# Weaving the last head's recurrence with the key and value expansion, in an order pinned on TensorE

## The chip, the cores and the metric

One NeuronCore of a Trainium2 chip runs the whole kernel. The metric is the device time of one execution in microseconds (us). Three runs of the kernel before took 884.52, 885.75 and 885.99, a median of 885.75.

## What is computed

One layer of a diffusion backbone over 640 tokens: 512 latent ones and 128 of context, five blocks of 128. One input projection feeds two groups of heads side by side. The part that matters here, shortened:

```python
hm, C_new, n_new, m_new = _mlstm_bidir(mq, mk, mv, gates_i, gates_f, ctx_C, ctx_n, ctx_m)   # 4 heads x 128
hm = _rmsnorm(hm, mlstm_norm_g) * sigmoid(mo)
ckv = _rmsnorm(kv_lat, kv_lora_g)                              # 256 wide
q = _mla_queries(q_lat, q_lora_g, w_q_up, q_head_g, rope)      # 384 wide -> 8 heads x 96
kv = (ckv @ w_kv_up).reshape(B, T, 8, 64 + 64)                 # the key and value expansion
k, v = rmsnorm(concat(kv[..., :64], k_rope)), kv[..., 64:]     # also for 128 cached context tokens
ha = _block_attention(q, k, v)
x = x + g1 * (concat(hm, ha) @ w_out)                          # then the feed-forward layer
```

The recurrence of a head is computed chunkwise: scores s of a block's keys with all queries, times decay weights W, give p; numerators are sums of p times v over blocks, forward and backward, and end in a normalised quotient hm. It does not depend on the expansion, nor the expansion on it.

## The kernel before

Weights and activations are split into a high and a low half, and three matmuls (high-high, high-low, low-high) make one product (`mm3`, L485-488). `split` (L108-110) makes the halves: a cast on ScalarE (L109) and a subtraction on VectorE (L110).

PSUM has two pools: psD, two buffers of two banks each (1024 columns), and psS, four buffers of one bank. A tile is written by TensorE and read by ScalarE and VectorE, and its buffer is then used again.

A framework orders the instructions: each engine has one queue, filled at build time by a list scheduler that takes whichever instruction is ready by its model, with the program's order as the priority. On the chip each engine takes its own queue strictly in order and waits at semaphores.

The stage around the change, in the program's order:

- `mlstm(h)` (L683-747): for j = 4 (context), 0, 1, 2, 3 the scores s (psS, three matmuls), for j < 4 the product c with the initial state (L716 scales it into the numerators num on ScalarE), the weights W (GpSimd adds the mask, L729; ScalarE takes exponentials, L730 and L732), p on VectorE (L739), and the forward numerator n (L698-706: matmuls L702, VectorE adds to num, L704, or ScalarE copies, L706). After the loop come the backward numerators.
- `context` (L749-764): a transpose pk, weighted keys kw on ScalarE (L757), the state pc (L760), its copy co and two output DMAs.
- `mlstm_end(h)` (L766-790): VectorE makes den (L770-772), hm in five blocks of 128 columns (L779, L780); ScalarE squares each with its sum (L781, into dg); VectorE scales the sums ssh (L782), GpSimd takes the root (rsh, L361), VectorE multiplies (L787), TensorE transposes (ht, hc, L788), VectorE multiplies by the output gate (L789, L790). It runs as a hook in `mlstm(h + 1)` after j = 0.
- After all four heads and `mlstm_end(3)`: the transposes ckt of the compressed latent and its halves kth and ktl (L806-815), then the expansion (L834-863): two halves hf of six tiles kvu of 128 tokens by 512 columns, six matmuls each, each tile in a psD buffer of its own. ScalarE copies the keys kn (L848), casts v (L109) or copies the context's v (L852), squares the keys (L854); VectorE makes the low half of v (L110) and sums the squares (L855). At the end of a half comes a reciprocal root on VectorE by iteration (L367-372).
- The query transposes qlt (L870), their split into qth and qtl, and the query product qu (L486-488). Strips of the modulation matrix w_ada (L389) fill TensorE from here on; their loads go through SyncE's queue in an order fixed at build time.

Of the kernel before, what the change touches and what calls it, by code (L numbers as in the profile page):

```python
# [19 lines left out]
P = 128  # L20
# [34 lines left out]
def hybrid_layer(ctx: ExitStack, tc: tile.TileContext, d, o):  # L55
# [429 lines left out]
    def mm3(out, lh, ll, rh, rl, start, stop):  # L485
        PE.matmul(out, lhsT=lh, rhs=rh, start=start, stop=False)  # L486
        PE.matmul(out, lhsT=lh, rhs=rl, start=False, stop=False)
        PE.matmul(out, lhsT=ll, rhs=rh, start=False, stop=stop)
# [194 lines left out]
    def mlstm(h, hook=None):  # L683
# [7 lines left out]
        def blk(dr, j, i):  # L691
            if i == 4:
                return pc_[:, dr, :]
            s0 = off[dr][j] + (i - j if dr == 0 else i) * P
            return pu[:, dr, s0:s0 + P]


        def numer(dr, i):  # L698
            js = [4] if i == 4 else (list(range(i + 1)) if dr == 0 else list(range(i, 4)))
            ps = psS(f"n{h}{i}{dr}")[:, 0:VC]  # L700
            for j in js:
                PE.matmul(ps, lhsT=blk(dr, j, i), rhs=mv32[:, j, h, :], start=j == js[0], stop=j == js[-1])  # L702
            if i < 4:
                V.tensor_tensor(out=num[dr][:, i, :], in0=ps, in1=num[dr][:, i, :], op=ALU.add)  # L704
            else:
                S.copy(num[dr][:, i, :], ps)  # L706

        wc = sm("wc", [P, 2], bufs=2)
        for j in (4, 0, 1, 2, 3):
            s_ps = psS(f"s{h}{j}")  # L710
            if j < 4:
                mm3(s_ps, kh[:, j * P:(j + 1) * P], kl_[:, j * P:(j + 1) * P], qh[:, 0:TL], ql_[:, 0:TL], True, True)
                pc = psS(f"c{h}{j}")[:, 0:260]
                mm3(pc, qh[:, j * P:(j + 1) * P], ql_[:, j * P:(j + 1) * P], ch, cl, True, True)
                for dr in range(2):
                    S.activation(out=num[dr][:, j, :], in_=pc[:, dr * 130:dr * 130 + VC], func=AF.Copy, scale=w_col[:, j, dr, h:h + 1])  # L716
            else:
                mm3(s_ps[:, 0:P], kh[:, TL:T], kl_[:, TL:T], qh[:, TL:T], ql_[:, TL:T], True, True)
# [21 lines left out]
            numer(0, j)  # L740
            if j == 4:
                numer(1, 4)
                context(h, kc, wc)
            if j == 0 and hook:
                hook()
        if h + 1 < MH:
            mlstm_loads(h + 1)
        for i in (3, 2, 1, 0):
            numer(1, i)  # L749
        fin[h] = (num, sg)  # L750

    def context(h, kc, wc):
        pk = psS(f"pk{h}")[:, 0:P]
        PE.transpose(out=pk, in_=kc, identity=ident)
# [4 lines left out]
        for dr in range(2):  # L759
            PE.matmul(pc[:, dr * 130:dr * 130 + VC], lhsT=kw[:, dr, :], rhs=mv32[:, 4, h, :], start=True, stop=True)  # L760
# [73 lines left out]
    for hf in range(2):  # L834
        ku = U(f"kn{hf}")
        kn = view(ku, 0, 6, 4, QK)
        vu = U(f"v{hf}", F32R)
        vv = view(vu, 0, 5, 4, P)
        hi, lo = wget(("kup", hf))
        ssk = sm("ssk", [P, 6, 4], bufs=1)  # L840
        rsk = sm("rsk", [P, 6, 4], bufs=1)
        for i in range(6):
            ps = psD(f"kvu{hf}{i}")[:, 0:512]
            for k in range(2):
                c = slice(k * 512, (k + 1) * 512)
                mm3(ps, kth[:, k, i * P:(i + 1) * P], ktl[:, k, i * P:(i + 1) * P], hi[:, c], lo[:, c], k == 0, k == 1)
            p4 = ps.rearrange("p (h c) -> p h c", h=4)
            S.copy(kn[:, i, :, 0:NOPE], p4[:, :, 0:NOPE])  # L848
            if i < 5:
                split(vv[:, i, :, 0:VD], vv[:, i, :, VD:P], p4[:, :, NOPE:P])  # L850
            else:
                S.copy(vctx[:, hf], p4[:, :, NOPE:P])  # L852
            sq = view(Pp(f"sqk{hf}{i}"), 0, 4, NOPE)
            S.activation(out=sq, in_=kn[:, i, :, 0:NOPE], func=AF.Square)  # L854
            V.tensor_reduce(out=ssk[:, i, :], in_=sq, axis=AX.X, op=ALU.add)  # L855
        V.tensor_tensor(out=ssk, in0=ssk, in1=ssr.unsqueeze(2).broadcast_to([P, 6, 4]), op=ALU.add)
        V.tensor_scalar(out=ssk, in0=ssk, scalar1=1.0 / QK, scalar2=EPS, op0=ALU.mult, op1=ALU.add)
        rsqrt_v(rsk.rearrange("p a b -> p (a b)"), ssk.rearrange("p a b -> p (a b)"))
        for k in range(4):
            G.tensor_tensor(out=kn[:, :, k, 0:NOPE], in0=kn[:, :, k, 0:NOPE], in1=rsk[:, :, k:k + 1].broadcast_to([P, 6, NOPE]), op=ALU.mult)  # L860
            G.tensor_tensor(out=kn[:, :, k, NOPE:QK], in0=krr, in1=rsk[:, :, k:k + 1].broadcast_to([P, 6, ROPE]), op=ALU.mult)
        kn_u.append(kn)
        v_u.append(vv)
# [551 lines left out]
```

## Time and profile before

| | us |
|---|---|
| median of 3 runs | 885.75 |
| profiled execution | 885.93 |
| its span | 883.8 |
| its time outside the span | 2.13 |

The first part of the page gives the busy time of each engine and its share of the span. A row of the windows has the stretch, its length, busy time and count of TensorE (PE), its weight loads (PEld), VectorE (DVE), ScalarE (ACT) and GpSimd (POOL), then the granted TensorE clock, where 1.00 is full, the DMA engines' busy share and GB/s. A row of the waits names the engine and line that waited, for whom, the total in us, how often, and the longest. A row of a timeline has its start from the span's beginning, its duration, engine, line, operation, output and inputs, shapes and how many alike stand in it (x5); in brackets stands the idle time of the engine before it and what ended it. TensorE overlaps its matmuls, so that they start closer together than one lasts.

### The profile page before, as it was taken

To read this page: it belongs to the slowest core of one execution; us is meant where nothing else is said; L and a number is where in the kernel's file an instruction comes from. 1 tells how busy PE (TensorE), PEld (TensorE's weight loads), DVE (VectorE), ACT (ScalarE), POOL (GpSimd) and SP (SyncE) were. 2 spreads that over 40 slices of the span, in tenths; PEclk is the share of its full clock that TensorE was granted. 3 is DMA by queue.
4 is the path that set the end of the run, shared out by engine and by line. 5 is a ranking of instruction groups with operands and counts; after the bars stand their busy time and mean duration, and the time that the engine had idled before them with its cause. 6 is when DMAs were issued, how large, how long until landed. Compare 5 with 4: busy or idle time off the path is not lost.

```text
span 883.8 us, 15202 instructions
## 1 busy us (share of the span) xinstructions
PE 856.6 (97%) x5805; PEld 801.8 (91%) x5805; DVE 615.9 (70%) x1226; ACT 436.6 (49%) x959; POOL 297.2 (34%) x301
## 2 busy tenths in 40 slices
PE   6999999999889999999989999999999999999998
PEld 5689889999778677889989999999999999999998
DVE  2654733646787889977898587595876949678663
ACT  3424425545864688955557253361544517254540
POOL 3100113322333576743753152241514215152300
PEclk9999999999999999999999999999999999999999
DMA  9742853231316200322141312122122221412132
GB/s 358 307 145 61 281 185 89 63 102 48 99 57 239 96 1 1 120 72 72 49 144 45 99 49 96 49 96 96 49 96 88 80 73 57 134 50 73 48 102 90
DMA packets 22328, 89.63 MB, mean 101 GB/s; under 512 B 3144, under 2 KB 3944, under 8 KB 18928
## 3 DMA queue, kind: packets, MB, share of 16 engines
q1 hardware_dynamic: 19440, 81.95, 26.8%
q0 software_dynamic: 1664, 4.26, 1.7%
q10 hardware_dynamic: 1152, 2.46, 0.7%
q8 instruction: 46, 0.75, 0.4%
q14 instruction: 26, 0.21, 0.1%
HBM read 85.33 MB, written 3.32 MB: 100 GB/s over the span
## 4 chain that ended last, share of the span: by engine, by line
PE 84%; DVE 8%; DMA 3%; ACT 3%; issue 1%; POOL 0%; SPq 0%; DVEq 0%; ACTq 0%; POOLq 0%
PE dn L637 25%; PE qk L637 6%; PE wo L637 5%; PE mo L637 3%; PE ada L389 2%; PE pv L1013 2%; DMA st<-in_w_ada 2%; PE n L702 2%; PE up8M L1235 1%; PE up12M L1235 1%; PE up13M L1235 1%; PE up15M L1235 1%; PE up14M L1235 1%; PE up11M L1235 1%; PE up9M L1235 1%; PE up7M L1235 1%
## 5 line engine op out<-in xcount | busy, mean ns | idle before, releaser
L109 ACT CAST wh<-st 128x1024 fp32r<-128x1024 f32 (+4 forms) x69 | 69.3, 1007 | 101.1 <-PE dn L637 32.9
L1118 DVE SCALAR_TENSOR_TENSOR xr<-dn,modT,xr 128x320 f32<-128x320 f32 x64 | 35.3, 551 | 107.3 <-PE dn L637 107.3
L637 PE MATMUL dn<-fh,wh 128*128 128x320 f32 x448 | 102.7, 310 | 0.2 <-ACT fh L1278 0.2
L110 DVE TENSOR_TENSOR wl<-st,wh 128x1024 fp32r<-128x1024 f32 (+4 forms) x67 | 83.3, 1246 | 27.8 <-ACT wh L109 26.8
L637 PE MATMUL dn<-fh,wl 128*128 128x320 f32 x448 | 102.0, 309 | 0.0
L637 PE MATMUL dn<-fl,wh 128*128 128x320 f32 x448 | 98.7, 309 | 0.0
L109 ACT CAST wu<-S 128x512 fp32r<-128x512 f32 x64 | 38.1, 616 | 98.5 <-issue 92.3
L637 PEld LDWEIGHTS dn<-fh,wh 128*128 128x128 f32 x448 | 74.8, 188 | 2.1 <-PE dn L637 1.6
L637 PEld LDWEIGHTS dn<-fh,wl 128*128 128x128 f32 x448 | 75.0, 188 | 0.0
L637 PEld LDWEIGHTS dn<-fl,wh 128*128 128x128 f32 x448 | 74.1, 188 | 0.0
L1273 POOL TENSOR_TENSOR r<-r,rbs 128x320 f32<-128x320 f32 x32 | 37.4, 1180 | 106.9 <-DVE r L1251 106.9
L110 DVE TENSOR_TENSOR wu<-S,wu 128x512 fp32r<-128x512 f32 x64 | 57.4, 906 | 1.1 <-ACT wu L109 0.9
L1277 ACT ACTIVATE r<-r 128x192 f32<-128x192 f32 (+2 forms) x96 | 40.8, 465 | 26.0 <-DVE r L1251 17.1
L729 POOL TENSOR_TENSOR W<-ngb,mask 128x128 f32<-128x128 f32 x40 | 19.5, 501 | 66.5 <-DVE p L739 33.2
L1280 DVE TENSOR_TENSOR fl<-r,fh 128x320 fp32r<-128x320 f32 x56 | 38.1, 699 | 3.0 <-ACT r L1279 3.0
L1004 POOL TENSOR_TENSOR tot<-tot,p 128x512 f32<-128x512 f32 x24 | 37.2, 1550 | 5.9 <-ACT p L986 3.9
L109 ACT CAST wu<-pair 128x512 fp32r<-128x512 f32 x24 | 14.1, 615 | 43.8 <-PE dn L637 41.6
L110 DVE TENSOR_TENSOR pu<-p,pu 128x512 fp32r<-128x512 f32 x32 | 33.0, 1046 | 2.5 <-ACT pu L109 2.5
L219 POOL TENSOR_TENSOR S<-st,st 128x512 f32<-128x512 f32 x8 | 13.0, 1627 | 60.1 <-DVE wu L110 60.1
L1013 PE MATMUL pv<-pu,v 128*128 128x512 f32 x80 | 29.1, 427 | 2.1 <-DVE pu L110 2.0
L637 PE MATMUL wo<-mh,wh 128*128 128x320 f32 x128 | 29.6, 311 | 0.7 <-DVE xr L1120 0.7
L637 PE MATMUL qk<-hh,wl 128*128 128x320 f32 x128 | 29.9, 312 | 0.0
(487 smaller groups left out, 2437.6 us busy)
## 6 DMA issues: line engine op xcount, KB each, us to landing
st<-in_w_ada SPq DMA_DIRECT2D x16, 1024.0 KB, 5.4
st<-in_w_down SPq DMA_DIRECT2D x32, 512.0 KB, 3.4
ad<-in_w_ada SPq DMA_DIRECT2D x8, 1024.0 KB, 17.2
st<-in_w_up SPq DMA_DIRECT2D x16, 512.0 KB, 3.7
pair<-in_w_up SPq DMA_DIRECT2D x16, 512.0 KB, 4.9
st<-in_w_qko SPq DMA_DIRECT2D x12, 512.0 KB, 3.6
st<-in_w_out SPq DMA_DIRECT2D x8, 512.0 KB, 3.5
x<-in_x SPq DMA_DIRECT2D x4, 640.0 KB, 6.8
```

Of the source, the lines that this page charges most:

```text
L109: S.copy(hi, src)
L110: return eng.tensor_tensor(out=lo, in0=src, in1=f(hi), op=ALU.subtract)
L389: PE.matmul(ps[32 * j:32 * j + 32, 0:n], lhsT=sz[:, 2 * q + k, :], rhs=w[:, k, c], start=q == 0, stop=q == 3, tile_position=(0, 32 * j))
L637: PE.matmul(out[:, hf * 512:hf * 512 + HT], lhsT=wt[:, c], rhs=xt[k][:, hf * HT:(hf + 1) * HT], start=k0 == 0 and n == 0, stop=k1 == nk an ...
L729: G.tensor_tensor(out=W[:, dg:dg + P], in0=nb_[dr][:, j * P:(j + 1) * P], in1=mask[:, dr, :], op=ALU.add)
L1004: G.tensor_tensor(out=tot[h], in0=first, in1=pj, op=ALU.add)
L1013: PE.matmul(pacc[h], lhsT=v_u[hf][:, j, hh_, :], rhs=w, start=j == 0 and k == 0, stop=j == 4 and k == 1)
L1118: V.scalar_tensor_tensor(out=xr[m][:, 0:HT], in0=ps[:, 0:HT], scalar=modT[:, gi_ + m, 0:1], in1=xr[m][:, 0:HT], op0=ALU.mult, op1=ALU.add)
L1235: PE.matmul(ps, lhsT=w[:, c], rhs=b[k], start=k == 0 and w is hi and b is bh, stop=k == 3 and w is lo)
L1273: E.tensor_tensor(out=t, in0=t, in1=rbs[:, c], op=ALU.mult)
L1277: S.activation(out=t[:, c0:c1], in_=t[:, c0:c1], func=AF.Relu, bias=r[n][:, w:w + 1])
L1280: V.tensor_tensor(out=FL[n][:, c], in0=t, in1=f(FH[n][:, c]), op=ALU.subtract)
```

## The change

The expansion becomes a generator, `expand()`, which stops after each tile. `mlstm` of the last head gets it as `fill` and takes one tile after each of its steps j = 4, 0, 1, 2, 3, and one in the backward numerators after i = 2. With `fill`, the forward numerator of a step is computed one step later (`due`); `context` is cut into `context` and `context_out`, and the second is another step later. `queued()` puts each of these matmul groups behind the one before it on TensorE (`issue_after`), so that the scheduler can't take them in another order; `line.clear()` ends that, and the remaining tiles follow without it. Two tiles share a double bank of psD, one in each half. ckt, krr and what belongs to them move ahead of the last head's recurrence in the program, `mlstm_end(3)` behind it.

```diff
-    def mlstm(h, hook=None):
+    line = {}
+
+    def queued():
+
+        return tc.issue_after(line["pe"].ins) if line else nullcontext()
+
+    def mlstm(h, hook=None, fill=None):
...
             ps = psS(f"n{h}{i}{dr}")[:, 0:VC]
-            for j in js:
-                PE.matmul(ps, lhsT=blk(dr, j, i), rhs=mv32[:, j, h, :], start=j == js[0], stop=j == js[-1])
+            with queued():
+                for j in js:
+                    last = PE.matmul(ps, lhsT=blk(dr, j, i), rhs=mv32[:, j, h, :], start=j == js[0], stop=j == js[-1])
+            if fill:
+                line["pe"] = last
...
         wc = sm("wc", [P, 2], bufs=2)
+        due = None
         for j in (4, 0, 1, 2, 3):
...
+            if due is not None:
+                numer(0, due)
+                if due == 4:
+                    numer(1, 4)
+                    kw = context(h, kc, wc)
+                elif due == 0:
+                    context_out(h, kw)
...
-            numer(0, j)
-            if j == 4:
-                numer(1, 4)
-                context(h, kc, wc)
+            if fill:
+
+                due = j
+                fill()
+            else:
+                numer(0, j)
+                if j == 4:
+                    numer(1, 4)
+                    context_out(h, context(h, kc, wc))
             if j == 0 and hook:
                 hook()
         if h + 1 < MH:
             mlstm_loads(h + 1)
+        if fill:
+            numer(0, due)
         for i in (3, 2, 1, 0):
             numer(1, i)
+            if fill and i == 2:
+                fill()
         fin[h] = (num, sg)
...
+        return kw
+
+    def context_out(h, kw):
         pc = psS(f"pc{h}")
...
-    for h in range(MH):
+    for h in range(MH - 1):
         mlstm(h, (lambda: mlstm_end(h - 1)) if h else None)
-        if h + 1 < MH:
-            head_in(h + 1)
-    mlstm_end(MH - 1)
+        head_in(h + 1)
...
-    for hf in range(2):
...
-        for i in range(6):
-            ps = psD(f"kvu{hf}{i}")[:, 0:512]
...
+    def expand():
+
+        for hf in range(2):
...
+            for i in range(6):
+                if i % 2 == 0:
+                    pair = psD(f"kvu{hf}{i}")
+                ps = pair[:, i % 2 * 512:i % 2 * 512 + 512]
+                with queued():
+                    for k in range(2):
+                        c = slice(k * 512, (k + 1) * 512)
+                        last = mm3(ps, kth[:, k, i * P:(i + 1) * P], ktl[:, k, i * P:(i + 1) * P], hi[:, c], lo[:, c], k == 0, k == 1)
+                if line:
+                    line["pe"] = last
...
+                if i < 5:
+                    yield
...
+    tiles = expand()
+    mlstm(MH - 1, lambda: mlstm_end(MH - 2), lambda: next(tiles))
+    line.clear()
+    mlstm_end(MH - 1)
+    for _ in tiles:
+        pass
```

What it does to the queues shows at three places. The names are the tiles of above with the head and step appended (s31 is the score of head 3, j = 1; ht2 and hc2 are the transposes of head 2's hm), wh and wl the halves of weights.

TensorE before, around the last transposes of head 2. Ahead of this piece stand seven tiles of the expansion (kvu00 to kvu05 and kvu10), head 3's s30, c30, context and first numerators, and the first three transposes, which come between kvu10 and kvu11.

```order
L486 MATMUL kvu11_2747<-wh32_2280,kth_2567 128x512
L487 MATMUL kvu11_2747<-wl32_2281,kth_2567 128x512
L488 MATMUL kvu11_2747<-wh32_2280,ktl_2568 128x512
L788 MATMUL ht2_2421<-ident_94,hm2_2400 128x128
L788 MATMUL hc2_2422<-ident_94,hm2_2400 128x128
L486 MATMUL s31_2435<-mqk3_2160 128x512
L487 MATMUL s31_2435<-mqk3_2160 128x512
L488 MATMUL s31_2435<-mqk3_2160 128x512
L486 MATMUL c31_2439<-chl3_2139,mqk3_2160 128x260
```

TensorE after, the same transposes. Ahead of this piece stand s34, the first tile, s30, c30, the numerators n340 and n341, and pk3; the second tile bears its pair's name, kvu00.

```order
L486 MATMUL kvu00_2413<-wh31_2221,kth_2336 128x512
L487 MATMUL kvu00_2413<-wl31_2222,kth_2336 128x512
L488 MATMUL kvu00_2413<-wh31_2221,ktl_2337 128x512
L828 MATMUL ht2_2494<-ident_94,hm2_2473 128x128 x4
L828 MATMUL hc2_2495<-ident_94,hm2_2473 128x128
L486 MATMUL s31_2508<-mqk3_2160 128x512
L487 MATMUL s31_2508<-mqk3_2160 128x512
L488 MATMUL s31_2508<-mqk3_2160 128x512
```

The transposes moved from around the eighth tile to behind the second, and the third to twelfth tile and all of the recurrence's steps from s31 on now stand behind them.

ScalarE before, from the first square (dg) of head 2 to the fourth of its five.

```order
L781 ACTIVATE dg_2403,ssh_2401<-hm2_2400 128x128
L716 ACTIVATE num30_2338<-c30_2377,cols_1009 128x129
L716 ACTIVATE num31_2339<-c30_2377,cols_1009 128x129
L781 ACTIVATE dg_2403,ssh_2401<-hm2_2400 128x128 x2
L848 COPY kn0_2615<-kvu02_2651 128x4x64
L109 CAST v0_2616<-kvu02_2651 128x4x64
L732 ACTIVATE W310_2445<-ngb0_2131,cols_1009 128x256
L762 COPY co_2369<-pc3_2366 128x2x129
L781 ACTIVATE dg_2403,ssh_2401<-hm2_2400 128x128
L732 ACTIVATE W311_2450<-ngb1_2133,cols_1009 128x128
L732 ACTIVATE W320_2469<-ngb0_2131,cols_1009 128x128
```

ScalarE after, from the copy of the second tile to the fifth square.

```order
L893 COPY kn0_2403<-kvu00_2413 128x4x64
L109 CAST v0_2404<-kvu00_2413 128x4x64
L821 ACTIVATE dg_2476,ssh_2474<-hm2_2473 128x128
L899 ACTIVATE sqk01_2465<-kn0_2403 128x256
L821 ACTIVATE dg_2476,ssh_2474<-hm2_2473 128x128 x2
L754 ACTIVATE W310_2528<-ngb0_2131,cols_1009 128x256
L754 ACTIVATE W311_2533<-ngb1_2133,cols_1009 128x128
L821 ACTIVATE dg_2476,ssh_2474<-hm2_2473 128x128
L752 ACTIVATE W310_2528<-W310_2528,cols_1009 128x128
L752 ACTIVATE W311_2533<-W311_2533,cols_1009 128x128
L821 ACTIVATE dg_2476,ssh_2474<-hm2_2473 128x128
```

The squares now stand closer together; the exponentials L754 and L752 of W310 and W311 (L732 and L730 before) stand between the third, the fourth and the fifth.

TensorE before, behind the last tile of the expansion: the query transposes qlt0 to qlt2, and ht3 and hc3, the transposes of head 3's hm.

```order
L870 MATMUL qlt0_2835<-ident_94,ql_u_1038 128x128 x5
L788 MATMUL ht3_2553<-ident_94,hm3_2532 128x128 x2
L870 MATMUL qlt1_2845<-ident_94,ql_u_1038 128x128 x5
L788 MATMUL ht3_2553<-ident_94,hm3_2532 128x128 x2
L788 MATMUL hc3_2554<-ident_94,hm3_2532 128x128
L870 MATMUL qlt2_2855<-ident_94,ql_u_1038 128x128 x5
```

TensorE after, the same piece; kvu14 is the pair of the last two tiles, and its second half stands here.

```order
L926 MATMUL qlt0_2829<-ident_94,ql_u_1038 128x128 x5
L828 MATMUL ht3_2707<-ident_94,hm3_2686 128x128 x4
L828 MATMUL hc3_2708<-ident_94,hm3_2686 128x128
L486 MATMUL kvu14_2781<-wh32_2280,kth_2336 128x512
L487 MATMUL kvu14_2781<-wl32_2281,kth_2336 128x512
L488 MATMUL kvu14_2781<-wh32_2280,ktl_2337 128x512
```

The last tile and the last two query transposes moved behind all of head 3's transposes.

## Rows read from the trace of the kernel before

**Rows 1.** The page: span, and busy time by engine.

```profile
span 883.8 us, 15202 instructions
PE 856.6 (97%) x5805; PEld 801.8 (91%) x5805; DVE 615.9 (70%) x1226; ACT 436.6 (49%) x959; POOL 297.2 (34%) x301
```

**Rows 2.** Windows: the stretch of the recurrence's first steps.

```profile
229.00:246.50 17.50, 14.84 (x76) 11.93 (x75) 14.08 (x51) 13.81 (x52) 5.41 (x9) 1.00 0.24 79
```

**Rows 3.** Waits of TensorE, 226 to 300 us.

```profile
PE kvu L486 <- DVE v L110: 2.8, 3, 1.3
PE pc L760 <- ACT kw L757: 1.4, 1, 1.4
...
PE qlt L870 <- ACT qlt L872: 0.6, 1, 0.6
PE ada L389 <- DMA st<-in_w_ada: 0.6, 2, 0.5
...
PE n L702 <- DVE p L739: 0.2, 1, 0.2
```

**Rows 4.** Timeline of TensorE, 229 to 267 us.

```profile
229.41 0.45 PE L486 MATMUL kvu<-wh,kth 128*128 128x512 f32 x1
...
232.68 0.27 PE L754 MATMUL pk<-ident,kc 128*128 128x128 f32 x1
...
234.60 0.48 PE L486 MATMUL s<-mqk 128*128 128x512 f32 x1
...
235.74 0.40 PE L486 MATMUL kvu<-wh,kth 128*128 128x512 f32 x1
...
244.67 0.49 PE L788 MATMUL ht<-ident,hm 128*128 128x128 f32 x3
...
265.55 0.44 PE L486 MATMUL qu<-wh,qth 128*128 128x384 f32 x1
```

**Rows 5.** Timeline of VectorE, 229.5 to 246 us.

```profile
233.26 1.06 DVE L779 TENSOR_SCALAR hm<-ck_u,den 128x128 f32<-128x128 f32 x5
234.24 0.42 DVE L110 TENSOR_TENSOR v<-kvu,v 128x256 fp32r<-128x256 f32 x1
...
236.02 0.60 DVE L780 SCALAR_TENSOR_TENSOR hm<-ck_u,den,hm 128x128 f32<-128x128 f32 x2
...
236.87 0.88 DVE L739 SCALAR_TENSOR_TENSOR p<-s,W 128x512 f32<-128x512 f32 x2
...
241.65 0.16 DVE L782 TENSOR_SCALAR ssh<-ssh 128x5 f32<-128x5 f32 x1
...
243.14 1.06 DVE L787 TENSOR_SCALAR hm<-hm,rsh 128x128 f32<-128x128 f32 x5
```

**Rows 6.** Timeline of ScalarE, 229.5 to 246 us.

```profile
232.21 0.37 ACT L848 COPY kn<-kvu 128x256 f32<-128x256 f32 x1 [2.06 <-PE kvu L488]
...
235.80 0.35 ACT L781 ACTIVATE dg<-hm 128x128 f32<-128x128 f32 x1
...
239.77 0.69 ACT L730 ACTIVATE W<-W,cols 128x128 f32<-128x128 f32 x2
```

**Rows 7.** Timeline of GpSimd, 229.5 to 246 us.

```profile
237.63 1.29 POOL L729 TENSOR_TENSOR W<-ngb,mask 128x128 f32<-128x128 f32 x3 [5.49 <-DVE p L739]
...
241.90 1.20 POOL L361 TENSOR_TENSOR rsh<-ssh,mhalf 128x5 f32<-128x5 f32 x1 [1.46 <-DVE ssh L782]
```

**Rows 8.** Windows: the end of the program.

```profile
880.00:882.50 2.50, 0.00 (x0) 0.00 (x0) 0.99 (x3) 0.00 (x0) 0.00 (x0) 1.00 0.37 131
882.50:883.80 1.30, 0.00 (x0) 0.00 (x0) 0.00 (x0) 0.00 (x0) 0.00 (x0) 0.53 0.00 0
```

**Rows 9.** Timeline of TensorE: strips at the start, and the last matmul.

```profile
16.44 3.64 PE L389 MATMUL ada<-ad,sz 128*32 128x256 f32 x32
...
22.79 1.93 PE L389 MATMUL ada<-ad,sz 128*32 128x256 f32 x32
...
879.51 0.31 PE L637 MATMUL dn<-f,wl 128*128 128x320 f32 x1
```

More of the change, by code (lines that the diff above doesn't have):

```diff
@@ L1 @@
-from contextlib import ExitStack
+from contextlib import ExitStack, nullcontext
 import numpy as np
@@ L487, in mm3 @@
         PE.matmul(out, lhsT=lh, rhs=rl, start=False, stop=False)
-        PE.matmul(out, lhsT=ll, rhs=rh, start=False, stop=stop)
+        return PE.matmul(out, lhsT=ll, rhs=rh, start=False, stop=stop)
     def group_n(keys, kts, ncol, name, nada=0):
@@ L711, in mlstm @@
             if j < 4:
-                mm3(s_ps, kh[:, j * P:(j + 1) * P], kl_[:, j * P:(j + 1) * P], qh[:, 0:TL], ql_[:, 0:TL], True, True)
-                pc = psS(f"c{h}{j}")[:, 0:260]
-                mm3(pc, qh[:, j * P:(j + 1) * P], ql_[:, j * P:(j + 1) * P], ch, cl, True, True)
+                with queued():
+                    mm3(s_ps, kh[:, j * P:(j + 1) * P], kl_[:, j * P:(j + 1) * P], qh[:, 0:TL], ql_[:, 0:TL], True, True)
+                    pc = psS(f"c{h}{j}")[:, 0:260]
+                    last = mm3(pc, qh[:, j * P:(j + 1) * P], ql_[:, j * P:(j + 1) * P], ch, cl, True, True)
+                if fill:
+                    line["pe"] = last
                 for dr in range(2):
@@ L717, in mlstm @@
             else:
-                mm3(s_ps[:, 0:P], kh[:, TL:T], kl_[:, TL:T], qh[:, TL:T], ql_[:, TL:T], True, True)
+                last = mm3(s_ps[:, 0:P], kh[:, TL:T], kl_[:, TL:T], qh[:, TL:T], ql_[:, TL:T], True, True)
+                if fill:
+                    line["pe"] = last
+            if due is not None:
[5 more added lines that the diff above has]
+                    context_out(h, kw)
             for dr in range(2):
@@ L753, in context @@
         pk = psS(f"pk{h}")[:, 0:P]
-        PE.transpose(out=pk, in_=kc, identity=ident)
+        with queued():
+            last = PE.transpose(out=pk, in_=kc, identity=ident)
+        if line:
+            line["pe"] = last
         kw = view(wwp.tile([P, 512], F32, tag="W", name=f"kw{h}"), 0, 2, P)
@@ L757, in context @@
             S.activation(out=kw[:, dr, :], in_=pk, func=AF.Copy, scale=wc[:, dr:dr + 1])
+        return kw
+    def context_out(h, kw):
         pc = psS(f"pc{h}")
-        for dr in range(2):
-            PE.matmul(pc[:, dr * 130:dr * 130 + VC], lhsT=kw[:, dr, :], rhs=mv32[:, 4, h, :], start=True, stop=True)
+        with queued():
+            for dr in range(2):
+                last = PE.matmul(pc[:, dr * 130:dr * 130 + VC], lhsT=kw[:, dr, :], rhs=mv32[:, 4, h, :], start=True, stop=True)
+        if line:
+            line["pe"] = last
         co = view(sm("co", [P, 260], bufs=1), 0, 2, 130)
@@ L832, in hybrid_layer @@
     V.tensor_copy(out=identr, in_=ident)
-    for hf in range(2):
[L835 to L841, printed above, removed]
-        for i in range(6):
-            ps = psD(f"kvu{hf}{i}")[:, 0:512]
[L844 to L863, printed above, removed]
```

30 lines of the change are left out of this document (added).

## The prediction

> **What bounds the kernel now.** The page's first part comes first: TensorE is busy 97% of the span [rows 1], so a change saves only where TensorE stands still, and costs wherever it newly does. The windows come next: of the 17.5 us from 229.0 TensorE works 14.84 [rows 2], so 2.66 us are idle at full clock. The waits of TensorE from 226 to 300 say for whom: the kv tiles for VectorE's low half of v, 2.8 us in three waits, pc for ScalarE's kw 1.4, the query transposes 0.6, a numerator 0.2, together 5.0, and weight strips for their DMA 0.6 [rows 3]. The timelines then give the dates. All this is what the change can win: 5.6 us of 885.93.
>
> **What moves.** TensorE takes its instructions in order, and that order is the one shown above: nothing later passes a waiting transpose. It differs from 229.4, the first kv tile, to about 296, and is the same behind. No matmul is added or removed: 72 matmuls of the twelve kv tiles, head 3's scores and numerators and the transposes only change places. So the sum is over waits.
>
> **A. The transposes of head 2, +6.2.** Before, eight kv tiles stand ahead of the last of these transposes, and they begin at 244.67 without a wait [rows 4]. Now two tiles stand there. When does TensorE arrive? Before, two tiles and the two context numerators take it from 229.41 to pk at 232.68, 3.27 us; s30 and c30 take from 234.60 to 235.74, 1.14 us [rows 4]. Now the same pieces and pk (0.3) lead up to ht2: 229.41 + 3.27 + 1.14 + 0.3 = 234.1, with 0.4 of small waits (under C) 234.5.
>
> When are its inputs there? VectorE began the five scalings hm at 233.26; now the v low half of the first tile, 0.42, stands ahead: 233.7, done by 234.7 (1.06 less the overlap); five accumulations at 0.26 (two took 0.60 with 0.08 of overlap) end at 236.0 [rows 5]. Then ScalarE squares the five blocks. In its new order two exponentials of W310 and W311 stand between the fourth square and the fifth, and they need GpSimd's masked sums. GpSimd started these 0.76 after VectorE's p had started (236.87 to 237.63) and took 1.29 for three [rows 5, 7]; p now starts at 236.0, since no tile's work stands between the accumulations, so the sums run from 236.8 to 238.0, the two exponentials after the second of them take 0.69 [rows 6] and end at 238.3, the last square, 0.35, and the read-out of its sum (0.2, an estimate) bring 238.9. From there the trace has the whole tail: ssh at 241.65, rsh at 241.90 for 1.20, hm times rsh at 243.14 [rows 5, 7], which is 1.49 from ssh to the scalings, and 0.3 until the first block is written (a fifth of their 1.06, and a signal). 238.9 + 1.49 + 0.3 = 240.7: TensorE stands from 234.5 to 240.7, **6.2 us**. If ScalarE took every square at once, the last would be done at 236.5, ht2 would start at 238.3, and the wait is 3.8: that is the low end. No reason leads below it, as the accumulations themselves end at 236.0. The high end is 7.0: ScalarE also casts, copies and squares the second tile in this stretch. I take 6.2. Behind ht2 stand s31, c31 and all the rest; nobody else fills the time, since tiles three to eight are queued behind it.
>
> **B. The waits of before, -5.0.** All of rows 3 but the DMA's go: the instructions that waited now stand elsewhere, with other suppliers.
>
> **C. New waits behind, +4.3.** The pairing looks like four buffers, but a tile is released as a whole: the second half of each double bank waits until VectorE has read the first. Ahead of ht2: pk 0.35 (ScalarE's copies of the numerators now come behind the first tile's kn, v and square) and the second tile 0.1. After ht2 the recurrence fills in well: only the fourth tile waits, 0.2. When the recurrence is out of steps, kvu13 waits for the v low half of kvu12, which stands on VectorE behind parts of two long chains, the root of the key norms and head 3's denominators: 0.9, the size that the same wait has (the kv row's 2.8 in three, the longest 1.3, mean 0.93). Head 3's transposes now stand ahead of kvu15 and wait 0.8 for the same kind of chain as head 2's; kvu15 0.2. qlt1 wants the double bank that kvu15 has just filled, so two ScalarE copies of 0.37 [rows 6] and their signals stand between: 0.9. The third query transpose and the first query tile wait for ScalarE's copies and casts: 0.9 together, where 0.6 was before. Sum 0.35 + 0.1 + 0.2 + 0.9 + 0.8 + 0.2 + 0.9 + 0.9 = 4.35, say 4.3. The low end is what the old order's tail had, one mean kv wait for each half and the query's: 0.93 + 0.93 + 0.6 = 2.4; the high end 5.5, if each of the last five is 0.25 longer. So the query product starts 6.2 - 5.0 + 4.3 = 5.5 after its 265.55 [rows 4], near 271.0.
>
> **D. Weight strips, -0.6.** The w_ada loads keep their time, since on SyncE's queue the next one even moves ahead of the load of w_q_up, while TensorE comes 5 us later: the two DMA waits, 0.6 [rows 3], are then over. From 0 to -0.6; I take -0.6.
>
> **E. TensorE's clock, +1.5.** [...]
>
> [...]
>
> **The sum.** 6.2 - 5.0 + 4.3 - 0.6 + 1.5 = 6.4 on the profiled execution's 885.93 (span 883.8 and 2.13 around it): 892.3. That execution is 0.18 above the median of 885.75, so I say **892.1**.
>
> **The rivals.**
> First, the clock stays up: all but E holds, 885.75 + 4.9 = **890.7**. For it: no dip between two matmuls in this trace. Against: a fall 2.7 us after the last one.
> [...]
> Third, ScalarE reaches the squares as they come: A is 3.8 and C 2.4: 3.8 - 5.0 + 2.4 - 0.6 = +0.6, **886.4**, with the clock's 1.5 **887.9**. For it: ScalarE is busy only 13.81 of the 17.5 us [rows 2]; against: two exponentials between the fourth square and the fifth.
> Fourth, the other side: the change does what its words say, the recurrence's steps cover the kv tiles' copies and head 2's end is covered as well. Then B and D go, C is at its low end, A is nothing: -5.0 - 0.6 + 2.4 = -3.2, **882.6**. It decides itself at one point: ht2 must be ready when TensorE arrives at 234.5, or the wait be under 3.2 us, where A - 5.0 - 0.6 + 2.4 turns negative. Against it: the accumulations ending at 236.0, with 1.20 of GpSimd and 0.35 of square yet to come. For it: only that dates which I moved by hand might be off by 1 to 2 us.
> Fifth, the pairs' halves are released apart, so that the change has four buffers: the waits of kvu01, 03, 13 and 15 go, 0.1 + 0.2 + 0.9 + 0.2 = 1.4: **890.7**, the same as the first and counted with it.
>
> **How the numbers follow.** Forecast 0.42 (its own range 890.9 to 893.6); first and fifth 0.22; second 0.14; third 0.16, half of it with the clock's price; fourth 0.06. A measurement of this kernel can tell 0.2%, 1.8 us, from no change: within are 884.0 to 887.5. Faster is the fourth, 0.06; the same is the third without the clock, 0.08; slower the rest, 0.86. For 8 in 10 the range runs from 887.6, the third with the clock, to 894.6, just above the second.
>
> **What would show it.** In the trace after: a wait of TensorE's ht transposes of about 6 us for VectorE's hm, beginning near 234.5; a granted clock under 1.00 in the window after it, and s31 and the next kv tiles longer than 0.40 a matmul; the three kv waits of 2.8 and pc's 1.4 absent; small waits of kvu13, ht3 and qlt1, each under 1; the first query matmul 5 to 7 us later than 265.55; no DMA wait of the strips before 296; everything after 300 only shifted. I am wrong if ht2 waits under 3.2 us, or if tiles of the weave stand between and shorten it; in size, if the clock stays at 1.00 through the gap.

## The result: 899.25 us, slower than forecast

The changed kernel takes 899.25 us (median of four runs, 897.55 to 900.04); the kernel before, in four runs on the same chip, 885.87 (884.52 to 886.92). The ratio is 1.0152, with an interval of 1.0135 to 1.0169. The forecast had the direction and the longest wait, but 892.1 us, and a range that ends at 894.6: of the 13.4 us lost it had foreseen 6.4.

The page of the changed kernel, to be held against [rows 1]:

```profile
span 896.8 us, 15201 instructions
PE 862.7 (96%) x5805; PEld 804.9 (90%) x5805; DVE 614.8 (69%) x1226; ACT 437.4 (49%) x959; POOL 299.5 (33%) x301
```

TensorE has the same 5805 matmuls, yet is busy 6.1 us longer, in a span 13.0 us longer. A busy time that grows without one more matmul says that some of them ran slower; the other 6.9 us are standing still.

The waits of TensorE from 226 to 315 us, against [rows 3] (total, times, longest):

```profile
PE ht L828 <- DVE hm L827: 7.1, 3, 6.0
PE qlt L926 <- ACT qlt L928: 1.0, 1, 1.0
PE ada L389 <- DMA st<-in_w_ada: 0.8, 1, 0.8
PE kvu L486 <- DVE v L110: 0.7, 1, 0.7
...
PE hc L828 <- DVE hm L827: 0.5, 1, 0.5
```

One wait of 6.0 for the scaled blocks hm of head 2 has come; of the kv tiles' 2.8 us for v 0.7 is left, and pc's 1.4 is gone. The weight strips still wait 0.8 for their DMA.

TensorE's timeline, against [rows 4]: the first tile, head 2's transposes and what follows them, and the tail up to the first query matmul:

```profile
230.39 0.45 PE L486 MATMUL kvu<-wh,kth 128*128 128x512 f32 x1
...
241.87 1.08 PE L828 MATMUL ht<-ident,hm 128*128 128x128 f32 x4 [6.01 <-DVE hm L827]
242.82 0.78 PE L486 MATMUL s<-mqk 128*128 128x512 f32 x1
...
248.27 0.40 PE L486 MATMUL s<-mqk 128*128 128x512 f32 x1
...
264.26 0.50 PE L486 MATMUL kvu<-wh,kth 128*128 128x512 f32 x1 [0.74 <-DVE v L110]
...
268.98 0.81 PE L828 MATMUL ht<-ident,hm 128*128 128x128 f32 x2 [0.61 <-DVE hm L827]
...
271.53 0.46 PE L828 MATMUL hc<-ident,hm 128*128 128x128 f32 x1 [0.47 <-DVE hm L827]
271.86 0.80 PE L486 MATMUL kvu<-wh,kth 128*128 128x512 f32 x1
...
275.53 0.77 PE L926 MATMUL qlt<-ident,ql_u 128*128 128x128 f32 x5 [0.74 <-ACT vctx L897]
277.26 0.77 PE L926 MATMUL qlt<-ident,ql_u 128*128 128x128 f32 x5 [0.96 <-ACT qlt L928]
278.01 0.45 PE L486 MATMUL qu<-wh,qth 128*128 128x384 f32 x1
```

Two things beside the waits: the first matmul of s31, behind the long wait, takes 0.78, where that of s32 takes 0.40; and the first of the last tile, at 271.86, is again as slow, 0.80, behind three waits of only half a microsecond. The windows show the granted clock there (the columns as in [rows 2]; the number behind the five engines is the clock):

```profile
229.00:241.00 12.00, 6.55 (x38) 4.87 (x36) 9.13 (x35) 9.50 (x35) 3.38 (x7) 0.99 0.28 104
241.00:250.00 9.00, 8.07 (x33) 6.96 (x33) 3.90 (x13) 3.89 (x13) 3.45 (x7) 0.63 0.05 17
250.00:260.00 10.00, 9.96 (x59) 8.78 (x60) 4.45 (x15) 4.66 (x15) 0.20 (x1) 1.00 0.00 0
...
268.00:272.00 4.00, 2.15 (x10) 0.98 (x8) 4.00 (x9) 0.89 (x3) 4.00 (x8) 0.95 0.00 2
272.00:276.00 4.00, 3.26 (x10) 2.16 (x11) 1.58 (x5) 1.59 (x4) 1.14 (x2) 0.62 0.00 0
```

The clock falls twice, to 0.50 for part of the windows at 0.63 and 0.62 (it reads 0.50 from 241.0 to 247.5 and from 272.0 to 275.0), and is back at 1.00 in between.

**Where the 13.0 us of span are.** Cut TensorE's time at three matmuls that every kernel has: the first kv tile, the first query matmul, and the feed-forward's first, up0M, which stands at 446.42 before and at 459.63 now. Up to the first tile +0.98 (228.3 to 231.2 in all the kernels below, with the same instructions ahead of it); the weave, from there to the first query matmul, 36.14 before and 47.62 now, +11.48; the query stage and attention +0.75; behind them -0.21. So the weave has it nearly all. In it TensorE's waits are 5.36 us more than before (10.46 for 5.10), and TensorE is at work 5.66 us longer (36.71 for 31.05): about half of the loss is standing still, the rest slower work.

### The profile page after: what moved, and what is told of

Same layout as the page of the kernel before. It is cut to its first block, busy times and chain, and to the rows that moved or that the text cites. A ratio compares the mean times of both kernels' runs of the same rounds, so it can differ in the third digit from the quotient of the medians.

```text
span 896.8 us, 15201 instructions
## 1 busy us (share of the span) xinstructions
PE 862.7 (96%) x5805; PEld 804.9 (90%) x5805; DVE 614.8 (69%) x1226; ACT 437.4 (49%) x959; POOL 299.5 (33%) x301
## 3 DMA queue, kind: packets, MB, share of 16 engines
q0 software_dynamic: 1664, 4.26, 1.5%
## 4 chain that ended last, share of the span: by engine, by line
PE 84%; DVE 7%; DMA 3%; ACT 3%; issue 2%; POOL 1%; SPq 0%; DVEq 0%; POOLq 0%; ACTq 0%
PE dn L637 25%; PE qk L637 6%; PE wo L637 5%; PE mo L637 2%; PE ada L389 2%; PE pv L1069 2%; DMA st<-in_w_ada 2%; PE n L709 2%; PE up12M L1291 1%; PE up8M L1291 1%; PE up4M L1291 1%; PE up14M L1291 1%; PE up3M L1291 1%; PE up13M L1291 1%; PE up11M L1291 1%
```

## The experiments

All are variants of the changed kernel, but the last. Each was profiled once and timed; the weave and the two stages are from the profile, "waits" is the sum of TensorE's waits in the weave (in e4 and e10 added matmuls stand where part of them was), the last column the ratio to before's runs on the same chip, with its interval. There before's medians were 885.58 to 886.74.

| kernel | weave | waits | query and attention | behind | median us | ratio |
|---|---|---|---|---|---|---|
| before | 36.14 | 5.10 | 180.87 | 437.4 | 885.87 | 1 |
| changed | 47.62 | 10.46 | 181.62 | 437.2 | 899.25 | 1.0152 [1.0135, 1.0169] |
| e1 keys late | 44.34 | 9.32 | 184.79 | 436.6 | 896.32 | 1.0102 [1.0066, 1.0138] |
| e3 ht2 late | 42.14 | 6.32 | 183.00 | 437.6 | 895.04 | 1.0096 [1.0063, 1.0129] |
| e4 filler | 45.48 | 6.12 | 181.78 | 438.7 | 898.14 | 1.0122 [1.0090, 1.0155] |
| e7 ht3 late | 47.56 | 11.87 | 181.57 | 437.3 | 897.93 | 1.0128 [1.0087, 1.0168] |
| e5 no pair | 42.28 | 9.02 | 182.23 | 437.6 | 893.68 | 1.0075 [1.0051, 1.0100] |
| e6 no pin | 40.01 | 7.86 | 181.50 | 436.3 | 890.54 | 1.0039 [1.0024, 1.0054] |
| e8 neither | 37.25 | 4.63 | 181.44 | 437.3 | 886.35 | 0.9999 [0.9983, 1.0015] |
| e9 no pair, ht2 late | 37.09 | 5.77 | 183.46 | 439.8 | 891.31 | 1.0048 [1.0030, 1.0065] |
| e10 waits alone | 42.18 | 3.11 | 181.71 | 440.6 | 895.91 | 1.0111 [1.0081, 1.0141] |
| e11 ht2 behind five | 35.52 | 4.48 | 183.78 | 439.0 | 887.48 | 1.0005 [0.9986, 1.0024] |
| e12 before, pc late | 36.11 | 4.48 | 181.23 | 436.4 | 887.51 | 0.9997 [0.9978, 1.0015] |

**e1: GpSimd's key scalings later.** The second fall begins where VectorE scales the five blocks of head 3. VectorE and GpSimd there, in the changed kernel:

```profile
241.44 1.07 DVE L827 TENSOR_SCALAR hm<-hm,rsh 128x128 f32<-128x128 f32 x5 [1.31 <-POOL rsh L361]
...
268.43 3.05 DVE L827 TENSOR_SCALAR hm<-hm,rsh 128x128 f32<-128x128 f32 x5
```

```profile
268.01 0.83 POOL L907 TENSOR_TENSOR kn<-kn,rsk 128x384 f32<-128x384 f32 x1
268.80 0.51 POOL L908 TENSOR_TENSOR kn<-krr,rsk 128x192 f32<-128x192 f32 x1
```

GpSimd's pair comes four times on end. The five take 3.05 for head 3 and 1.07 for head 2, at 241.44. The experiment holds the first half's key scalings back until head 3's product mix_m is written (rsk gets a second buffer for it).

```diff
-            for k in range(4):
-                G.tensor_tensor(out=kn[:, :, k, 0:NOPE], ...rsk...)
+            def keys(kn=kn, rsk=rsk):
+                for k in range(4):
+                    G.tensor_tensor(out=kn[:, :, k, 0:NOPE], ...rsk...)
+            if hf == 0:
+                held.append(keys)
+            else:
+                keys()
...
     mlstm_end(MH - 1)
+    first = G.tensor_tensor(out=mark, in0=mix_m[:, MH - 1, T - 1:T], ...)
+    with tc.issue_after(first.ins):
+        held[0]()
```

> The changed kernel (899.25 us) with one thing moved: GpSimd's eight scalings of the first half's keys (L907, L908) stand behind a one-column add that reads head 3's gated output, so they start after head 3's transposes and no longer beside VectorE's five scalings of head 3's hm. Theory (GpSimd's two-input operations hold up VectorE's scalings): the five take 1.06 us and not 3.05, the three waits of ht3 and hc3 (0.61, 0.47, 0.47) shrink to under 0.7 together, the last kv tile starts about 2 us sooner, and if TensorE's clock stays up there it is 1.3 us shorter: 896.0 to 897.4 us. Rival (the scalings wait for their own inputs, or the place of the transposes is what costs): 899.0 to 899.5 us, five scalings still at about 3 us.

VectorE in e1, a subtraction for the low half of a weight, which now meets the moved work, and TensorE's head 3 transposes, last tile and second query transpose:

```profile
273.17 1.44 DVE L110 TENSOR_TENSOR wl<-st,wh 128x768 fp32r<-128x768 f32 x1 [1.40 <-ACT wh L109]
```

```profile
268.93 0.92 PE L828 MATMUL ht<-ident,hm 128*128 128x128 f32 x4 [0.39 <-DVE hm L827]
...
270.05 0.51 PE L486 MATMUL kvu<-wh,kth 128*128 128x512 f32 x1
...
272.45 0.76 PE L938 MATMUL qlt<-ident,ql_u 128*128 128x128 f32 x5 [0.74 <-ACT vctx L899]
```

The five scalings, at 268.60, are back at 1.06 and head 3's transposes wait 0.39 once. The weave is 3.28 shorter: that is what this neighbourhood costs. The marks of the two kernels divide it. From the first query transpose to the last tile it is 2.27 (from 267.78) instead of 4.26 (from 267.60): 1.99 are the held-up scalings. From the last tile to the second query transpose, which waits 0.74 in both, it is 2.40 instead of 3.67: 1.27 are the second fall. But the clock falls all the same, only later: e1's first 4 us of query matmuls run at 0.57 (the window is shown under e9), and the query stage is 3.2 longer, 1.5 of it because the weight strips now wait 2.3 for their DMA instead of 0.8, the rest because TensorE is busy 1.6 longer. So the spans of the two profiles hardly differ, 896.3 and 896.8; the median falls by 2.9, and the intervals of the two ratios just touch. The two engines keep colliding too: the subtraction at 273.17, beside the key scalings, takes 1.44 instead of the 0.96 that it takes in the changed kernel, at 276.24, where GpSimd has nothing to do.

**e3: head 2's transposes after s32.** Only TensorE's transposes and the two products behind them move from s30 to s32; VectorE's part stays.

```diff
-    def mlstm_end(h):
+    def mlstm_end(h, apart=False):
...
+        def turn():                            # the five transposes, pinned, and mix_m
...
-                hook()
+                turn = hook()
+            if fill and j == 2:
+                turn()
```

> The changed kernel with head 2's five transposes pinned on TensorE behind the fourth kv tile, not behind the second; the vector work of head 2's end stays at its place in the program. Theory (TensorE stands because these transposes are in front, and the stand brings its clock down): the 6.0 us wait shrinks to under 2.5, the granted clock stays at 1.00 from 241 to 250, and the time falls by 6 to 8.5 us: 890.8 to 893.3 us. Rival (the recurrence behind waits for the same VectorE and ScalarE work, so the idle time is only dealt out to other waits): 897 us or more.

TensorE in e3, head 2's transposes, and two windows:

```profile
243.15 0.92 PE L834 MATMUL ht<-ident,hm 128*128 128x128 f32 x4 [0.61 <-DVE hm L828]
```

```profile
241.00:250.00 9.00, 8.39 (x47) 6.80 (x48) 5.41 (x17) 4.70 (x15) 1.50 (x2) 1.00 0.01 2
...
260.00:270.00 10.00, 6.77 (x22) 4.01 (x21) 7.31 (x18) 4.23 (x10) 5.86 (x9) 0.69 0.00 1
```

The wait goes from 6.01 to 0.61, the first fall with it, and the weave is 5.48 shorter, although the scaled blocks themselves come later (242.81, 13.9 after the first tile, instead of 11.05): TensorE, going on, gives VectorE other work first. The second fall stays (0.69) and reaches into the query stage. The median, 895.04, lies above what the theory allowed.

**e4: the wait kept, TensorE kept busy in it.** 22 matmuls into the bank that the transposes will overwrite stand ahead of them; their product is used nowhere.

```diff
+        if line:
+            with queued():
+                for _ in range(22):
+                    last = PE.matmul(pt, lhsT=kth[:, 0, 0:P], rhs=kth[:, 0, 0:512], start=True, stop=True)
+            line["pe"] = last
```

> The changed kernel with 22 more matmuls of 128x512 into the bank of head 2's transposes, directly ahead of these: their results are overwritten, so they only keep TensorE at work during the wait. At 0.23 us each they take 5.1 of the 6.0 us. Theory (the clock falls because TensorE stands): the transposes start when they did, the granted clock stays at 1.00, the matmuls of s31 to the third kv tile are issued 0.23 apart and not 0.43, and the time falls by 2.0 to 2.6 us: 896.7 to 897.3 us. Rival (the matmuls behind the wait are slow for another reason, or the clock falls all the same): 899 us or more.

TensorE in e4: the filler, the transposes, s31, s32.

```profile
235.02 5.19 PE L828 MATMUL ht<-kth 128*128 128x512 f32 x22
241.13 0.92 PE L833 MATMUL ht<-ident,hm 128*128 128x128 f32 x4 [0.92 <-DVE hm L832]
242.06 0.47 PE L486 MATMUL s<-mqk 128*128 128x512 f32 x1
...
245.26 0.40 PE L486 MATMUL s<-mqk 128*128 128x512 f32 x1
```

From s31 to s32 it takes 3.20 instead of 5.45, at a clock of 1.00: the first fall costs 2.25 us, and the weave is 2.14 shorter. The median, 898.14, lies between what the theory and its rival allowed. It fell by 1.1 only; in e4's profile the part behind attention is 1.5 longer.

**e10: both together.** e1's edit, e4's filler, and seven more such matmuls at the end of the weave (three behind the last tile, four behind the second query transpose): the clock reads 1.00 in every window from 229 to 300, the order and its suppliers stay.

```diff
+    lastp = idle_work(tail["pe"], 3)
...
+        if k == 1:
+            idle_work(turned, 4)
```

> The changed kernel with what the prediction mis-sized taken out, and its waits kept: GpSimd's scalings of the keys late (as in e1), 22 matmuls ahead of head 2's transposes (as in e4), and 3 and 4 such matmuls into an unread bank around the second query transpose, where TensorE waits for ScalarE. Theory (the clock and the held-up scalings are all that was missed; the prediction's waits of 5.5 us more than before are right): clock at 1.00 from 229 to 290, the first query matmul 41.6 to 42.5 us after the first kv tile (36.1 before, 47.6 in the changed kernel), 891 to 893.5 us. Rival (other losses in the weave): 43.5 us or more.

The window of e10 from the first query matmul, at 271.42:

```profile
271.30:275.30 4.00, 4.00 (x40) 2.44 (x39) 3.86 (x9) 3.11 (x5) 3.40 (x5) 1.00 0.60 170
```

The weave is 42.18. So the four kernels make a square: without the first fall -2.14 (e4) or -2.16 (e10 against e1), without the key scalings in the way -3.28 (e1) or -3.30 (e10 against e4). The 11.48 us of the weave are 2.15 of the first fall, 3.3 of the key scalings with the second fall, and 6.0 that stay with the clock up and the scalings free, which are the new order's waits in the main; for them the prediction had 6.2 - 5.0 + 4.3 = 5.5. The median, 895.91, is well above the forecast of it: behind attention the profile has 3.4 more than the changed kernel's, which none of the edits touch (see the last section).

**e7: head 3's transposes behind the last tile.** The rival to e1: not VectorE, but the place of the transposes.

```diff
-    mlstm_end(MH - 1)
+    turn = mlstm_end(MH - 1, True)
     for _ in tiles:
         pass
+    with tc.issue_after(tail["pe"].ins):
+        turn()
```

> The changed kernel with head 3's five transposes pinned behind the last kv tile, not ahead of it; nothing else moves. Theory (VectorE, held up by GpSimd, is what is late there): the last kv tile then waits for the v low half of the tile before it, which stands behind the same five scalings on VectorE, and starts no sooner than 271: 898.6 to 900.2 us. Rival (the place of head 3's transposes on TensorE is the cost, as the prediction had it): the 1.5 us of their waits go and the last tile runs at full clock, 896.5 to 897.5 us.

The last kv tile in e7:

```profile
269.79 0.80 PE L486 MATMUL kvu<-wh,kth 128*128 128x512 f32 x1 [3.50 <-DVE v L110]
```

The wait moves to the tile, as its buffer is freed by a v that stands on VectorE at 269.32, behind the same five scalings (3.05 from 266.35). The weave is 0.06 shorter. The median, 897.93, lies between the two forecasts; the wait in the trace decides for VectorE.

**e5 and e6: one half of the change each.** e5 gives every tile a double bank of its own; e6 takes the pins away, and the scheduler orders TensorE.

```diff
-                if i % 2 == 0:
-                    pair = psD(f"kvu{hf}{i}")
-                ps = pair[:, i % 2 * 512:i % 2 * 512 + 512]
+                ps = psD(f"kvu{hf}{i}")[:, 0:512]
```

```diff
-        return tc.issue_after(line["pe"].ins) if line else nullcontext()
+        return nullcontext()
```

> The changed kernel with only the pairing undone: each kv tile again has a psD buffer of its own; the weave and the pinned order stay. The order then puts head 3's transposes behind the first query tile, and GpSimd's scalings of the keys ahead of head 3's root. Theory (the end of the expansion costs 3.7 us more than the prediction had because the pairs put head 3's transposes ahead of the last tile and beside the scalings): the 6.0 us wait of head 2's transposes stays, with the fall of the clock behind it, but no ht3 wait, five scalings of head 3's hm at 1.1 us, no second fall of the clock, and the first query matmul 4 to 5 us earlier after the first kv tile than the 47.6 of the changed kernel: 894.0 to 896.0 us. Rival (the double bank with two tiles does hide evacuations): more kv waits, 899 us or more.

> The changed kernel with only the pinning undone: the weave and the pairs stay, the scheduler orders TensorE. It puts seven tiles ahead of head 2's transposes again. Theory (the pinned order is what lets TensorE reach these transposes too early): their wait is under 1 us, the clock is 1.00 to 260, and the time falls by 8 us or more from 899.25, to 887 to 891 us, the rest being the pairs' waits. Rival (the weave itself, not the pin, is what costs): 895 us or more.

TensorE in e5, and the longest kv wait and the clock beside it in e6:

```profile
240.12 1.09 PE L828 MATMUL ht<-ident,hm 128*128 128x128 f32 x4 [6.01 <-DVE hm L827]
```

```profile
234.73 0.72 PE L486 MATMUL kvu<-wh,kth 128*128 128x512 f32 x1 [1.99 <-DVE v L110]
```

```profile
234.00:241.00 7.00, 6.01 (x18) 4.47 (x18) 3.40 (x10) 5.39 (x23) 0.87 (x2) 0.76 0.00 1
```

Without the pairs the 6.01 stays and the weave is 5.34 shorter (4.73 together with the query stage and attention): GpSimd's key scalings are over (at 269.00) when head 3's five scalings begin (at 271.31), these take 1.06, there is no second fall, and head 3's transposes have moved out of the weave among the first query matmuls. The median, 893.68, is 0.3 below what the theory allowed. Without the pins the long wait goes, and five kv waits of 5.6 together come in its place, with a fall of the clock behind the longest, which the theory had not. So the pins make the long wait; with them, the pairs make the trouble at the end; and either alone makes the kernel slower, by 0.75% (6.6 us) for the pins without pairs and 0.39% (3.5) for the pairs without pins.

**e8: neither.** Both edits together; what is left is the woven order of the code.

> The changed kernel with pinning and pairing undone: what stays is the weave in the program's order and the numerators and the context's state one step later. TensorE's order is nearly that before, but with pc behind the first numerator. Theory (of the change only the lag saves something: pc's wait of 1.4 us for kw): the other waits as before, the first query matmul 35.0 to 36.2 us after the first kv tile (36.1 before): 884.3 to 886.0 us. Rival (the weave in the program's order, which moves head 3's end and the vector work, costs): 888 us or more.

The kv tile's wait in e8:

```profile
236.97 0.72 PE L486 MATMUL kvu<-wh,kth 128*128 128x512 f32 x1 [2.03 <-DVE v L110]
```

pc's wait of 1.4 is gone, this one is there instead, and the clock falls behind it (0.86 over 229 to 241, the tile's matmuls 0.63 each where they take 0.39 from 240.73 on): the weave is 1.11 longer than before's, which the theory had not. The time is that of before. Weaving by itself wins nothing.

**e9: no pair, and head 2's transposes late.** The edits of e5 and e3: what the order could give without the faults found so far.

> The changed kernel with the pairing undone and head 2's transposes pinned behind the fourth kv tile. The two costs found, the wait for head 2 with its clock and the end of the expansion, are then both out. Theory (these two are all that makes the changed kernel slower): the first query matmul 36 to 39 us after the first kv tile, clock at 1.00 throughout, 885.5 to 888.5 us. Rival (something else in the weave costs several us): 891 us or more.

The 4 us ahead of the first query matmul (at 265.43 in e9, 265.55 in before), in e9 and in before, and the 4 us from it, in e9 and in e1:

```profile
261.30:265.30 4.00, 2.20 (x16) 1.49 (x14) 2.36 (x5) 3.81 (x7) 3.88 (x5) 1.00 0.07 10
265.30:269.30 4.00, 3.87 (x15) 3.66 (x16) 3.71 (x15) 2.22 (x4) 0.00 (x0) 0.57 0.35 125
```

```profile
261.40:265.40 4.00, 3.36 (x25) 2.58 (x23) 3.35 (x10) 3.55 (x8) 0.79 (x1) 1.00 0.00 0
```

```profile
274.80:278.80 4.00, 4.00 (x32) 2.18 (x32) 3.86 (x9) 3.13 (x5) 3.40 (x5) 0.57 0.39 135
```

Head 2's transposes wait 1.98. The weave, 37.09, came out as hoped, the time did not: 891.31, 2.8 us above the top of what was expected. The bill comes in the query stage. Where TensorE was busy 3.36 of the 4 us ahead of it before, it is busy 2.20 in e9, the last two query transposes waiting 0.19 and 0.97 and the first query matmul 0.77; then the clock stands at 0.57, and 15 matmuls pass in 4 us, where e5, with the same order there and the clock at 1.00, has 24 (its window is shown in the last section). Head 3's transposes also stand among the query matmuls now. Query and attention take 2.6 us more than before. In e5 they take 1.4 more without the fall, so of the 2.6 about 1.2 are the fall's and the rest the order's. Behind them it is 2.4 more.

**e11: the same, with head 2's transposes after s33, and head 3's root behind the last key scaling.**

```diff
-            if fill and j == 2:
+            if fill and j == 3:
                 turn()
...
-    mlstm_end(MH - 1)
+    with tc.issue_after(scaled[0].ins):
+        mlstm_end(MH - 1)
```

> From the changed kernel: no pairs, head 2's transposes pinned behind the fifth kv tile, head 3's root on GpSimd pinned behind the scalings of the first half's keys. Theory (the costs found are out; what stays are evacuation waits like those before): no wait of head 2's transposes above 0.3, the first query matmul 35 to 36.5 us after the first kv tile, 884 to 887 us, that is at most 1 us better than the kernel before. Rival (the weave gains nothing, since the same ScalarE and VectorE work is waited for elsewhere): 888 us or more.

The window of e11 from the first query matmul, at 266.70:

```profile
266.60:270.60 4.00, 3.90 (x15) 3.61 (x16) 3.95 (x15) 2.20 (x4) 0.34 (x1) 0.60 0.35 125
```

Head 2's transposes wait for nothing any more. The weave is 35.52, 0.62 shorter than before's, the only one that is so by more than 0.03. The query stage takes it back as in e9: it is 2.9 longer than before's, with the clock at 0.60 behind the query transposes. 887.48, half a microsecond above what was expected, is no difference to before.

**e12: the kernel before, with only pc moved.** Head 3's context product goes behind s30, so that it need not wait for ScalarE's kw.

```diff
-                context(h, kc, wc)
+                kw = context(h, kc, wc)
+                if h < MH - 1:
+                    context_out(h, kw)
+            elif j == 0 and h == MH - 1:
+                context_out(h, kw)
```

> The kernel before with one part of the change: head 3's pc one step later, behind its first numerator. Its 1.4 us wait for kw goes. Theory (behind it TensorE meets the same ScalarE and VectorE chain at the kv tiles, so the wait moves): a kv wait of 1 to 2 us takes its place, the first query matmul 35.3 to 36.5 us after the first kv tile, 885 to 887.5 us. Rival (the 1.4 us are won): 34.9 us or less, 883.5 to 884.8 us.

The longest of the kv waits in e12:

```profile
255.99 0.50 PE L486 MATMUL kvu<-wh,kth 128*128 128x512 f32 x1 [1.47 <-DVE v L110]
```

pc waits no more, the kv waits grow from 2.8 in three to 3.6 in four, and the weave is 36.11 for 36.14. The wait belongs to VectorE's supply of v, not to the place of pc. No variant beats the kernel before.

## Why the prediction was right in direction and wrong in size

**A, the transposes of head 2, +6.2: right.** 6.01, and the transposes started 11.5 after the first tile (230.39 to 241.87), where the prediction had 11.3 (229.41 to 240.7). VectorE, ScalarE and GpSimd went through the steps as worked out, the last square behind two exponentials of W included. ScalarE in the changed kernel, these exponentials and the last square:

```profile
238.95 0.68 ACT L752 ACTIVATE W<-W,cols 128x128 f32<-128x128 f32 x2
239.54 0.29 ACT L821 ACTIVATE dg<-hm 128x128 f32<-128x128 f32 x1
```

e3 shows that the place makes the wait. In e4, where TensorE is at work meanwhile, the transposes start 11.2 after the first tile: their inputs come hardly earlier.

**B, -5.0, and C, +4.3: the sum about right, one term not, and that is the first step that failed.** The waits of the weave grew by 5.36, where 5.5 was said; with the clock up and the scalings free (e10) the weave is 6.0 longer. That the sum of the waits fits is partly luck. pk's wait was 0.3, kvu13's 0.74 of 0.9, the second query transpose's 0.74 of 0.9, the third's 0.96 of the 0.9 that it was to share with the first query tile, and three small ones (0.1, 0.2, 0.2) did not come. The failed term is ht3's, 0.8: with hc3's it was 0.61 + 0.47 + 0.47, since the blocks had to wait for one scaling after another, and the last tile came 1.99 later than with the scalings free (e1). The step behind it took head 3's five scalings for 1.06, like head 2's, and looked only for VectorE's own chain. The neighbour on GpSimd was missed, though before had a pair of rows that shows the effect, of head 1's four scalings on VectorE and of GpSimd beside them:

```profile
211.41 1.87 DVE L787 TENSOR_SCALAR hm<-hm,rsh 128x128 f32<-128x128 f32 x4
```

```profile
212.08 0.92 POOL L729 TENSOR_TENSOR W<-ngb,mask 128x128 f32<-128x128 f32 x2
```

Four scalings beside GpSimd (which issued a DMA of L764 until 212.05 and then made these sums) took 1.87, five alone 1.06 [rows 5]. Head 3's five scalings agree: 3.05 us for five, 0.61 each, beside GpSimd's 0.83 and 0.51, and 1.06, 0.21 each, in e1, where GpSimd is still. How one engine holds up the other is not shown; that it does, these rows show, and so the new neighbourhood was a thing to look for.

**E, the clock, +1.5: the second step that failed.** It reckoned with one fall, after the one long wait. No run shows the term of 1.5, which was the author's estimate: the slow strips at the start [rows 9] stand at a granted clock of 1.00 in before's trace (16 to 24 us), so they price no fall. In its place the runs showed 2.25 for the fall behind the long wait (e4), 2.15 of the weave. The second was not thought of at all: it cost 1.27 in the weave (e1), and it comes behind a stretch without any wait above 0.74 us. The reasoning knew only the end of the program, where the clock fell 2.7 us after the last matmul (879.82 to 882.5) [rows 8, 9], and took this for the only way to lose it. What brought the second fall is not shown: ahead of it TensorE was busy 2.15 of 4 us in several short pieces, and 0.62 followed; e5, with the same 2.15, keeps 1.00.

**D, -0.6: wrong, by little.** The weight strips still wait 0.8 at 307.81, although TensorE comes 12 us later.

**The gap closed.** In the span, 13.0 came where 6.4 was said. The weave was to be 5.5 + 1.5 = 7.0 longer and is 11.48: 3.3 for the key scalings (2.0) and the second fall (1.3), 0.65 for the first fall's price (2.15 for 1.5), 0.5 for the rest of the new order (6.0 for 5.5). Behind the first query matmul it is +0.54 where D said -0.6, another 1.14; and 0.98 lie ahead of the first tile, a size by which this place varies between the kernels' profiles. 3.3 + 0.65 + 0.5 + 1.14 + 0.98 = 6.6.

**The rivals.** The clock did not stay up (the first). The second, at 894.4, with 3.2 for the clock, came nearest, by luck: no run shows that price; the one fall that it reckoned with cost 2.15, both together 3.4, and it had no held-up scalings. ScalarE did not take the squares as they came (the third): the last stood behind two exponentials. Cover for head 2's end (the fourth) was not there. Pairs released by halves (the fifth) are ruled out by kvu13's wait of 0.74 at 264.26, which is for VectorE's v of kvu12, the first half of its own pair. The low end of the range, 887.6, was named as the third with the clock, which the working puts at 887.9.

## What to carry to other kernels

Pinning an order on an engine fixes who waits, and a chain of four engines that was hidden under eight tiles is in the open when two stand there: walk the chain to its end before choosing the place. Price a gap on TensorE at the gap and the slower matmuls behind it (6.01 and 2.15 here), and look for a fall of the clock behind many short gaps in a row as well (1.27 of the weave here, though in e5 such gaps brought none). When instructions move in time, look at what VectorE and GpSimd run side by side in the new order (five scalings took 3.05 for 1.06), and judge a change by the stage behind it too: e11 won 0.62 in its stage and gave back 2.9 in the next.

## What the hardware showed that was not expected

**The clock falls without a long wait.** In the 4 us up to the fall TensorE was busy 2.15 (changed), 2.20 (e9), 2.29 (e1) and 1.99 (e11), no wait above about one microsecond. It is no certainty: e5 has 2.15 of 4 us at the same place, and its clock stays at 1.00. Nor is one wait of middling length: behind 1.99 us (e6) and 2.03 (e8) the clock fell, behind 1.98 (e9) it did not. e5's 4 us ahead of the first query matmul, at 271.09, and from it:

```profile
267.00:271.00 4.00, 2.15 (x16) 1.44 (x14) 2.41 (x5) 3.85 (x7) 3.87 (x5) 1.00 0.08 10
271.00:275.00 4.00, 3.91 (x24) 3.74 (x25) 4.00 (x16) 2.18 (x4) 0.00 (x0) 1.00 0.36 125
```

**The same place, another clock.** From 445 to 475 us, the start of the feed-forward, which no variant touches, the clock is 1.00 in the profiles of before, changed, e1, e4, e6, e7, e8 and e12, 0.94 in e3, e5 and e10, and 0.89 in e9 and e11. Before and e9:

```profile
445.00:475.00 30.00, 26.74 (x182) 25.96 (x181) 26.44 (x46) 17.18 (x37) 16.66 (x17) 1.00 0.27 98
```

```profile
445.00:475.00 30.00, 27.35 (x165) 26.56 (x164) 23.25 (x41) 15.07 (x32) 16.17 (x15) 0.89 0.30 106
```

In the table the stretch behind attention is 436.3 to 437.6 in most, 439.0 to 440.6 in e9, e10 and e11, but 437.6 in e3 and e5, and 438.7 in e4 at a clock of 1.00. So the clock explains part of it at most. What decides the fall there, and what the rest is, stays open; single executions of the kernel before lie between 883.9 and 890.9, so the medians of the variants carry about this much that is not theirs, and their stretches in the weave are the surer measure.

**GpSimd is held up as well.** In e1 GpSimd's instruction at 273.75, beside VectorE's subtraction (273.17 to 274.61), takes 1.23 instead of 0.51, and the one at 276.23 takes 1.49 instead of 0.83.
